# Hybrid GDN and MoBA layer: the keys of four heads in the first phase, and beta's and the decay's columns in the delta rule's gate

## Chip, cores and metric

The kernel runs on one core of a Trainium2 chip. The metric is device time in microseconds (us). Three executions of the kernel before took 785.45 to 785.89 us, median 785.75.

## The reference, cut to what matters

One layer: RMS norm of x (256 positions, 2048 channels, float32), one wide input projection, two token mixers (a gated delta rule with 8 heads of 128, and block attention with 8 heads of 128), their gates, a merge, an output projection, a norm and the residual. The change touches only the input side of the delta rule:

```python
SPLITS = (3 * GDN_WIDTH, GDN_WIDTH, GDN_HEADS, GDN_HEADS, 3 * MOBA_WIDTH, MOBA_WIDTH, D_MODEL, D_MODEL)
proj = h @ w_in
gdn_qkv, gdn_z, gdn_b, gdn_a, ... = jnp.split(proj, offsets, axis=-1)
qkv = jax.nn.silu(causal_depthwise_conv(gdn_qkv, conv_w))
beta = jax.nn.sigmoid(gdn_b)
g = -jnp.exp(a_log) * jax.nn.softplus(gdn_a + dt_bias)
oa = gated_delta_rule(qa, ka, va, beta, g)          # chunks of 64
oa = rms(oa) * gdn_norm_w * jax.nn.silu(gdn_z)
```

In w_in the 1024 columns of the gate z are followed directly by the 8 columns of beta and the 8 of the decay.

## The kernel before, in words

All matrix products with weights are done in three parts: a float32 weight tile is split into hi (a copy on ScalarE, L223) and lo (raw minus hi, on VectorE, L224), both in the fp32r format, and the input, transposed to hT, is kept as hi and lo too. TensorE (PE) adds hi by hi, hi by lo and lo by hi. `mm` (L140) and `tr` (L143) are the helpers through which every product and transpose goes, so all have these two lines; `pin` keeps them in the program's order, while the framework's scheduler may move unpinned instructions of the other engines.

`proj_n` makes a block of 512 output columns: positions on partitions, 16 input tiles (k) of 128 channels, two position halves, three products each: 96 products of 512 columns. `proj_t` makes two heads, channels on partitions: 16 tiles, two heads, one product of 512 columns (hi of the weight by hi and lo of the input) and one of 256: 64 products.

The first phase (up to L341) loads x and w_in's columns for the keys and queries of heads 0 and 1 in five pieces (CHUNKS: 2, 2, 4, 4, 4 tiles), transposes x (`turn`), scales it by the pre-norm weight into hT (`turned`), and multiplies the pieces as they land (`first_split`, `first_products`). `stats` sums x squared. A few products of ones (WARM, WARM2) run ahead of them. After the phase, pba multiplies hT by the 16 columns of beta and the decay, which came by their own transfer (wba) and stand split in a 64-column tile. a_log and dt_bias are broadcast from memory over 128 partitions; a part of the identity is written to memory (ident_d) and read back spread over partitions into tv, as the start of the inverse.

Then `ORDER` lists the blocks: mv, mk are attention, kq the keys and queries of two delta-rule heads, v their values, zg and zm the two gates, ga and gb the merge gates. In each block `tick` is called after every six products (proj_n) or four pairs (proj_t). A tick advances queues of generators, in which all other work waits: a step runs, then yields how many blocks of two ticks to wait. The delta rule's queue (gq) holds, one after the other, `decays` (softplus and cumulative sums pg, a write g_d and broadcast grow, exponentials of differences dec), `scores` of eight heads (11 ticks each), `inverse` (63 steps on VectorE, slower while a v block is recent) and `solve`. The first merge-gate block gb0 drains this queue when it ends.

VectorE, ScalarE, GpSimd (POOL) and SyncE (SP) issue in their own order. SP issues the weight loads, POOL the small and rearranging transfers. Raw weight tiles have three buffers, splits three, PSUM four banks for blocks (acc) and four for the rest (aux).

Of the kernel before, what the change touches and what calls it, by code (L numbers as in the profile page):

```python
# [15 lines left out]
P = 128  # L16
# [3 lines left out]
WARM = 4  # L20
# [4 lines left out]
D_WAIT = 3.5  # L25
# [14 lines left out]
    "mv0 kq1 kq2 zg0 kq3 zg1 v0 v1 v2 ga0 zm0 zm1 ga1 mv1 v3 ga2 ga3 mk0 mk1 gb0 mk2 gb1 mk3 gb2 gb3"  # L40
# [31 lines left out]
def hybrid_layer(  # L72
# [31 lines left out]
    CB = 4 * GW  # L104
    CMQ = CB + 2 * H
# [43 lines left out]
    CHUNKS = (0, 2, 4, 8, 12, KT)  # L149
    NCH = len(CHUNKS) - 1  # L150
    KC = 4
    pre = big.tile([P, KT * nba + P], F32, tag="ga", name="pre")
    wba = pre[:, : KT * nba].rearrange("p (k c) -> p k c", c=nba)
    prow = pre[:, KT * nba :]
    nrow = cst.tile([KT, P], F32, name="nrow")
    nc.gpsimd.dma_start(nrow, pre_norm_w.rearrange("o (k p) -> (o k) p", p=P))
    xs = [big.tile([P, D], F32, tag=("z0", "z1")[t], name=f"x_{t}") for t in range(NT)]
    FIRST = (("k", CK), ("q", CQ))
    rawf = {n: big.tile([P, KT, 256], F32, tag=f"g{i}", name=f"rawf_{n}") for i, (n, _) in enumerate(FIRST)}
    for c in range(NCH):  # L160
        cs = slice(CHUNKS[c] * P, CHUNKS[c + 1] * P)
        for t in range(NT):
            nc.sync.dma_start(xs[t][:, cs], xf[t * P : (t + 1) * P, cs])
        for n, col in FIRST:
            nc.sync.dma_start(
                rawf[n][:, CHUNKS[c] : CHUNKS[c + 1]], w_in[cs, col : col + 256].rearrange("(k p) c -> p k c", p=P)
            )
    nc.sync.dma_start(wba, w_in[:, CB : CB + nba].rearrange("(k p) c -> p k c", p=P))

# [10 lines left out]
    nc.gpsimd.dma_start(prow[0 : NTAP * NCV, :], conv_w.rearrange("o t (m p) -> (o t m) p", p=P))  # L180
    nc.gpsimd.dma_start(prow[NTAP * NCV : NTAP * NCV + 1, :], gdn_norm_w)
    na = cst.tile([P, H], F32, name="na")
    nc.gpsimd.dma_start(na, a_log.broadcast_to([P, H]))
    dtb = cst.tile([P, H], F32, name="dtb")
    nc.gpsimd.dma_start(dtb, dt_bias.broadcast_to([P, H]))
    wbs = big.tile([P, KT, 64], F32R, tag="tt", name="wbs")
    nc.gpsimd.memset(wbs.bitcast(F32), 0.0)
# [22 lines left out]
    sel = cst.tile([64, nba], F32, name="sel")  # L210
    ident_d = dram.tile([64, 64], F32, name="ident_d")
    nc.gpsimd.dma_start(ident_d, ident[0:64, 0:64])
# [20 lines left out]
    pfirst = {n: [acc_tile(f"a_{n}0_{m}") for m in range(2)] for n, _ in FIRST}  # L233

    def turn(c):

        ks = range(CHUNKS[c], CHUNKS[c + 1])
        each = 1 if len(ks) == 2 else 2
        pts = []
        for i, k in enumerate(ks):  # L240
            if i % each == 0:
                pt = aux_tile(f"hTp_{k}")
            pts.append(pt[:, (i % each) * S : (i % each + 1) * S])
            for t in range(NT):
                tr(pts[-1][:, t * P : (t + 1) * P], xs[t][:, k * P : (k + 1) * P], ident)
        return [(k, pts[i]) for i, k in enumerate(ks)]

    def turned(pts):
        for i in range(0, len(pts), 2):
            for k, pr in pts[i : i + 2]:  # L250
                pin(nc.scalar.activation(hT[:, k, :S], pr, AF.Copy, scale=ncol[:, k : k + 1]))
            for k, pr in pts[i : i + 2]:
                pin(
                    nc.vector.scalar_tensor_tensor(
                        hT[:, k, S:], pr, ncol[:, k : k + 1], hT[:, k, :S].bitcast(F32), op0=ALU.mult, op1=ALU.subtract
                    )
                )

# [13 lines left out]
    def first_split(n, c):  # L272
        hi = wspl.tile([P, KC, 256], F32R, tag="hi", name=f"hi_{n}0_{c}")
        lo = wspl.tile([P, KC, 256], F32R, tag="lo", name=f"lo_{n}0_{c}")
        for u in range(0, CHUNKS[c + 1] - CHUNKS[c], 2):
            us = slice(u, u + 2)
            raw = rawf[n][:, CHUNKS[c] + u : CHUNKS[c] + u + 2]
            pin(nc.scalar.copy(hi[:, us, :], raw))
            pin(nc.vector.tensor_tensor(lo[:, us, :], raw, hi[:, us, :].bitcast(F32), op=ALU.subtract))
        return hi, lo  # L280

    def first_products(n, c, hi, lo):
        for kk in range(CHUNKS[c + 1] - CHUNKS[c]):
            k = CHUNKS[c] + kk
            for m in range(2):
                ms = slice(m * P, (m + 1) * P)
                pt = pfirst[n][m]
                mm(pt, hi[:, kk, ms], hT[:, k, :], start=(k == 0), stop=False)
                mm(pt[:, :S], lo[:, kk, ms], hT[:, k, :S], start=False, stop=(k == KT - 1))

    pts = turn(0)
# [3 lines left out]
    turned(pts)  # L295
    for i in range(WARM2):
        mm(warm[:, :P], ones, ones, start=True, stop=True)
    sk_ = first_split("k", 0)
    for c in range(NCH):
        first_products("k", c, *sk_)  # L300
        if c == 0:
            pts = turn(1)
        sq_ = first_split("q", c)
        if c + 1 < NCH:
            turned(pts)
            sk_ = first_split("k", c + 1)
        if c > 1:
            stats(c - 2)
        first_products("q", c, *sq_)
        if c + 2 < NCH:  # L310
            pts = turn(c + 2)
    stats(3)

    pin(nc.scalar.copy(wbs[:, :, 0:nba], wba))
    pin(nc.vector.tensor_tensor(wbs[:, :, 32 : 32 + nba], wba, wbs[:, :, 0:nba].bitcast(F32), op=ALU.subtract))
    nc.vector.memset(sel, 0.0)
    nc.vector.tensor_copy(sel[0:nba, :], ident[0:nba, 0:nba])
    nc.vector.tensor_copy(sel[32 : 32 + nba, :], ident[32 : 32 + nba, 32 : 32 + nba])
# [23 lines left out]


# [18 lines left out]
    def proj_n(w, col, stat, nk, name):  # L362

        pts = [acc_tile(f"a_{name}_{t}") for t in range(NT)]
        for kb in range(nk // 4):
            raw = wraw.tile([P, 4, 512], F32, tag="raw", name=f"raw_{name}_{kb}")
            nc.sync.dma_start(raw, w[kb * 512 : (kb + 1) * 512, col : col + 512].rearrange("(k p) c -> p k c", p=P))
            for u in range(2):
                hi, lo = split(raw[:, 2 * u : 2 * u + 2, :], [P, 2, 512], f"{name}_{kb}_{u}")
# [12 lines left out]
    ba = big.tile([64, 2 * S], F32, tag="tv", name="ba")  # L382
    nc.scalar.copy(ba, pba[0:64, :])
# [9 lines left out]
    def decays():  # L393
        pbt = aux_tile("pbt")
        for t in range(NT):
            for half in range(2):
                o_ = half * S + t * P
                mm(
                    pbt[:, t * nba : (t + 1) * nba], ba[:, o_ : o_ + P], sel, start=(half == 0), stop=(half == 1)
                )  # L400
        zz = cst.tile([P, NT, H], F32, name="zz")
        sp = cst.tile([P, NT, H], F32, name="sp")
        for t in range(NT):
            pa_ = pbt[:, t * nba + H : (t + 1) * nba]
            pin(nc.vector.scalar_tensor_tensor(zz[:, t, :], pa_, rstd[:, t : t + 1], dtb, op0=ALU.mult, op1=ALU.add))
        for t in range(NT):
            pb_ = pbt[:, t * nba : t * nba + H]
            pin(nc.scalar.activation(beta[:, t, :], pb_, AF.Exp, scale=nrstd[:, t : t + 1]))
# [13 lines left out]
        for y in late:  # L422
            pin(nc.scalar.activation(y, y, AF.Silu))
# [50 lines left out]
    def conv_silu(y, m, late=None):  # L474
# [8 lines left out]
        if late is None:  # L483
            nc.scalar.activation(y, y, AF.Silu)
        else:
            late.append(y)
# [94 lines left out]
    def silu_gate(n, col, c):  # L581
        pts = proj_n(w_in, col + c * 512, hT, KT, f"{n}{c}")
        for t in range(NT):
            nc.scalar.activation(
                z_tiles[n]()[:, t, c * 512 : (c + 1) * 512], pts[t], AF.Silu, scale=rstd[:, t : t + 1]
            )

    def keys_queries(p):
        h = 2 * p
        pk = pfirst["k"] if h == 0 else proj_t(CK + h * P, f"k{h}")  # L590
        kTs = [halves(pk[m], f"k{h + m}") for m in range(2)]
        if h == 0:
            qTs = [halves(pfirst["q"][m], f"q{h + m}") for m in range(2)]
            gq.add(decays())
        for m in range(2):
            conv_silu(kTs[m], H + h + m, None if h else late)
        if h:
            pq = proj_t(CQ + h * P, f"q{h}")
            qTs = [halves(pq[m], f"q{h + m}") for m in range(2)]
        for m in range(2):  # L600
            conv_silu(qTs[m], h + m, None if h else late)
        for m in range(2):
            gq.add(scores(h + m, kTs[m], qTs[m]))
# [509 lines left out]
```

## Time and profile before

| What | us |
|---|---|
| median of three executions | 785.75 |
| the profiled execution | 785.95 |
| its span, first to last instruction | 784.2 |
| first product of the first phase | 6.89 |
| first product of the first mv block | 40.83 |
| first block of the branch outputs (ua), in the chain | 599.93 |

The profiled execution's time holds 1.75 us outside the span. In the profile, PE is TensorE's products, PEld its weight loads, DVE is VectorE, ACT ScalarE, POOL GpSimd; SPq is SyncE's queue. A row of a group of instructions names line, engine, operation, output and inputs, then shape, count, busy time and mean ns of one. Products overlap in the pipeline, so the distance between two starts, and not the mean duration, is what one costs.

### The profile page before, as it was taken

To read this page: it belongs to the slowest core of one execution; us is meant where nothing else is said; L and a number is where in the kernel's file an instruction comes from. 1 tells how busy PE (TensorE), PEld (TensorE's weight loads), DVE (VectorE), ACT (ScalarE), POOL (GpSimd) and SP (SyncE) were. 2 spreads that over 40 slices of the span, in tenths; PEclk is the share of its full clock that TensorE was granted. 3 is DMA by queue.
4 is the path that set the end of the run, shared out by engine and by line. 5 is a ranking of instruction groups with operands and counts; after the bars stand their busy time and mean duration, and the time that the engine had idled before them with its cause. 6 is when DMAs were issued, how large, how long until landed. Compare 5 with 4: busy or idle time off the path is not lost.

```text
span 784.2 us, 10150 instructions
## 1 busy us (share of the span) xinstructions
PE 771.6 (98%) x3869; PEld 647.9 (83%) x3869; DVE 531.9 (68%) x875; ACT 413.3 (53%) x624; POOL 26.2 (3%) x53
## 2 busy tenths in 40 slices
PE   8999999999999999999999999999999999999995
PEld 6878888888888888888888888888888888888884
DVE  4877886785867898874346466554645668986673
ACT  5777665554745545455354646454464445465451
POOL 3010000100110000020000000000000000000000
PEclk9999999999999999999999999999999999999999
DMA  8857655665596656686445465556456555577542
GB/s 261 261 160 215 189 187 165 197 189 162 175 267 218 213 163 212 190 235 191 117 127 163 160 214 161 169 165 204 162 166 230 195 185 206 196 271 268 167 156 107
DMA packets 95248, 149.77 MB, mean 191 GB/s; under 512 B 5152, under 2 KB 47184, under 8 KB 94560
## 3 DMA queue, kind: packets, MB, share of 16 engines
q1 hardware_dynamic: 92000, 136.46, 54.5%
q0 software_dynamic: 2624, 11.63, 5.2%
q10 hardware_dynamic: 576, 1.05, 0.4%
q8 instruction: 30, 0.49, 0.3%
q14 instruction: 18, 0.15, 0.1%
HBM read 145.95 MB, written 3.17 MB: 190 GB/s over the span
## 4 chain that ended last, share of the span: by engine, by line
PE 94%; DVE 2%; SPq 1%; ACT 1%; DMA 1%; issue 0%; DVEq 0%; ACTq 0%
PE a_ga L140 11%; PE a_gb L140 11%; PE a_y L140 11%; PE a_mk L140 6%; PE a_v L140 6%; PE a_mq L140 6%; PE a_zg L140 6%; PE a_zm L140 6%; PE a_q L140 5%; PE a_k L140 5%; PE a_ub L140 5%; PE a_mv L140 5%; PE a_ua L140 5%; PE sv L140 2%; PE s L140 1%; DMA x<-in_x_dram 1%
## 5 line engine op out<-in xcount | busy, mean ns | idle before, releaser
L140 PE MATMUL a_ga<-hi_ga,hT 128*128 128x512 f32 x256 | 82.2, 394 | 0.0
L140 PE MATMUL a_gb<-hi_gb,hT 128*128 128x512 f32 x256 | 82.1, 394 | 0.0
L224 DVE TENSOR_TENSOR lo_gb<-raw_gb,hi_gb 128x1024 fp32r<-128x1024 f32 x32 | 39.2, 1224 | 41.1 <-ACT hi_gb L223 41.1
L223 ACT CAST hi_gb<-raw_gb 128x1024 fp32r<-128x1024 f32 x32 | 33.7, 1052 | 48.5 <-PE a_gb L140 34.5
L224 DVE TENSOR_TENSOR lo_ga<-raw_ga,hi_ga 128x1024 fp32r<-128x1024 f32 x32 | 39.0, 1223 | 29.2 <-ACT hi_ga L223 29.1
L223 ACT CAST hi_ga<-raw_ga 128x1024 fp32r<-128x1024 f32 x32 | 33.5, 1050 | 46.1 <-PE a_ga L140 30.3
L140 PEld LDWEIGHTS a_ga<-hi_ga,hT 128*128 128x128 f32 x256 | 48.1, 188 | 11.0 <-issue 1.0
L140 PEld LDWEIGHTS a_gb<-hi_gb,hT 128*128 128x128 f32 x256 | 48.1, 188 | 10.0
L140 PE MATMUL a_ga<-lo_ga,hT 128*128 128x512 f32 x128 | 50.0, 391 | 0.0
L140 PE MATMUL a_gb<-lo_gb,hT 128*128 128x512 f32 x128 | 49.8, 389 | 0.0
L140 PE MATMUL a_k<-hT,hi_k 128*128 128x512 f32 x128 | 46.8, 406 | 0.1
L140 PE MATMUL a_mk<-hT,hi_mk 128*128 128x512 f32 x128 | 46.1, 401 | 0.0
L140 PE MATMUL a_mq<-hT,hi_mq 128*128 128x512 f32 x128 | 45.7, 400 | 0.0
L140 PE MATMUL a_y<-hi_y,mT 128*128 128x512 f32 x144 | 45.6, 390 | 0.0
L140 PE MATMUL a_q<-hT,hi_q 128*128 128x512 f32 x128 | 45.6, 397 | 0.0
L140 PE MATMUL a_v<-hT,hi_v 128*128 128x512 f32 x128 | 45.3, 397 | 0.0
L140 PE MATMUL a_ua<-hi_ua,oaT 128*128 128x512 f32 x128 | 41.8, 395 | 0.0
L140 PE MATMUL a_zg<-hi_zg,hT 128*128 128x512 f32 x128 | 40.6, 391 | 0.0
L140 PE MATMUL a_zm<-hi_zm,hT 128*128 128x512 f32 x128 | 40.6, 392 | 0.0
L140 PE MATMUL a_mv<-hi_mv,hT 128*128 128x512 f32 x128 | 40.5, 392 | 0.0
L140 PE MATMUL a_ub<-hi_ub,obT 128*128 128x512 f32 x128 | 40.0, 389 | 0.0
L140 PE MATMUL a_k<-hT,lo_k 128*128 128x256 f32 x128 | 36.4, 284 | 0.0
(333 smaller groups left out, 1906.5 us busy)
## 6 DMA issues: line engine op xcount, KB each, us to landing
raw_ga<-in_w_in_dram SPq DMA_DIRECT2D x16, 1024.0 KB, 5.2
raw_gb<-in_w_in_dram SPq DMA_DIRECT2D x16, 1024.0 KB, 5.1
raw_y<-in_w_out_dram SPq DMA_DIRECT2D x15, 1024.0 KB, 5.0
raw_mv<-in_w_in_dram SPq DMA_DIRECT2D x8, 1024.0 KB, 5.6
raw_zg<-in_w_in_dram SPq DMA_DIRECT2D x8, 1024.0 KB, 5.1
raw_v<-in_w_in_dram SPq DMA_DIRECT2D x8, 1024.0 KB, 5.7
raw_zm<-in_w_in_dram SPq DMA_DIRECT2D x8, 1024.0 KB, 5.3
raw_mq<-in_w_in_dram SPq DMA_DIRECT2D x8, 1024.0 KB, 5.7
```

The costliest lines, as they stand in the source:

```text
L140: return pin(nc.tensor.matmul(*args, **kwargs))
L223: nc.scalar.copy(hi, raw)
L224: nc.vector.tensor_tensor(lo, raw, hi.bitcast(F32), op=ALU.subtract)
```

## The change

The first phase loads the keys of heads 0 to 3 (512 columns) instead of keys and queries of heads 0 and 1, in four pieces of four tiles each; x lands in pieces of 512 columns, the keys one tile of 128 rows and 512 columns per transfer. The number of the phase's products is the same: 64 of 512 columns and 64 of 256. Queries of heads 0 and 1, and 2 and 3, become blocks q0 and q1 of the order. pba and what fed it are gone: the gate zg is made in three blocks of 348, 348 and 344 columns, the last of which holds the gate's last 328 columns and the 16 of beta and the decay. This third block runs first, ahead of the order, in aux banks, and `decays` reads its last columns. a_log and dt_bias are one row, spread over partitions by a product with ones. tv is made by GpSimd (a memset and four selects). The small loads move from GpSimd's queue to SP's, nrow ahead of x and the others behind the keys. WARM is 6 instead of 4, D_WAIT 7 instead of 3.5.

```diff
-WARM = 4
+WARM = 6
-D_WAIT = 3.5
+D_WAIT = 7
-    "mv0 kq1 kq2 zg0 kq3 zg1 v0 v1 v2 ga0 zm0 zm1 ga1 mv1 v3 ga2 ga3 mk0 mk1 gb0 mk2 gb1 mk3 gb2 gb3"
+    "q0 mv0 zg0 q1 kq2 kq3 zg1 v0 v1 v2 ga0 zm0 zm1 ga1 mv1 v3 ga2 ga3 mk0 mk1 gb0 mk2 gb1 mk3 gb2 gb3"
...
+    ZG = (0, 348, 696, GW + nba)
+    ZW, ZBA = ZG[3] - ZG[2], GW - ZG[2]
+    NCH = KT // 4
-    nc.gpsimd.dma_start(nrow, pre_norm_w.rearrange("o (k p) -> (o k) p", p=P))
+    nc.sync.dma_start(nrow, pre_norm_w.rearrange("o (k p) -> (o k) p", p=P))
+    rawk = [big.tile([P, KT // 2, 512], F32, tag=f"g{i}", name=f"rawf_k{i}") for i in range(2)]
     for c in range(NCH):
-        cs = slice(CHUNKS[c] * P, CHUNKS[c + 1] * P)
         for t in range(NT):
+            cs = slice(c * 512, (c + 1) * 512)
             nc.sync.dma_start(xs[t][:, cs], xf[t * P : (t + 1) * P, cs])
-        for n, col in FIRST:
-            nc.sync.dma_start(
-                rawf[n][:, CHUNKS[c] : CHUNKS[c + 1]], w_in[cs, col : col + 256].rearrange("(k p) c -> p k c", p=P)
-            )
-    nc.sync.dma_start(wba, w_in[:, CB : CB + nba].rearrange("(k p) c -> p k c", p=P))
+        for k in range(4 * c, 4 * c + 4):
+            nc.sync.dma_start(rawk[k // 8][:, k % 8], w_in[k * P : (k + 1) * P, CK : CK + 512])
...
-    nc.gpsimd.dma_start(na, a_log.broadcast_to([P, H]))
-    nc.gpsimd.dma_start(dtb, dt_bias.broadcast_to([P, H]))
+    adrow = cst.tile([1, nba], F32, name="adrow")
+    nc.sync.dma_start(adrow[:, :H], a_log)
+    nc.sync.dma_start(adrow[:, H:], dt_bias)
-    nc.gpsimd.dma_start(ident_d, ident[0:64, 0:64])
...
+    def first_split(k, n):
+        hi = wspl.tile([P, 2, 512], F32R, tag="hi", name=f"hi_k0_{k}")
+        lo = wspl.tile([P, 2, 512], F32R, tag="lo", name=f"lo_k0_{k}")
+        raw = rawk[k // 8][:, k % 8 : k % 8 + n]
+        pin(nc.scalar.copy(hi[:, :n], raw))
+        pin(nc.vector.tensor_tensor(lo[:, :n], raw, hi[:, :n].bitcast(F32), op=ALU.subtract))
+        return [(k + i, hi[:, i], lo[:, i]) for i in range(n)]
+    def first_products(parts):
+        for k, hi, lo in parts:
+            for part in range(2):
+                for m in range(4):
+                    ms, pt = slice(m * P, (m + 1) * P), pfirst[m]
+                    if part == 0:
+                        mm(pt, hi[:, ms], hT[:, k, :], start=(k == 0), stop=False)
+                    else:
+                        mm(pt[:, :S], lo[:, ms], hT[:, k, :S], start=False, stop=(k == KT - 1))
...
+    turned(pts[:2])
+    parts = first_split(0, 1) + first_split(1, 1)
+    turned(pts[2:])
+    parts += first_split(2, 2)
     for c in range(NCH):
+        first_products(parts[4 * c : 4 * c + 2])
+        if c + 1 < NCH:
+            turned(turn(c + 1))
         if c == 0:
+            parts += first_split(4, 2)
+        stats(c)
+        first_products(parts[4 * c + 2 : 4 * c + 4])
+        for k in (4 * c + 6, 4 * c + 8):
+            if k < KT:
+                parts += first_split(k, 2)
-    pba = aux_tile("pba")
-    for k in range(KT):
-        mm(pba[0:64, :], wbs[:, k, :], hT[:, k, :], start=(k == 0), stop=(k == KT - 1))
...
+    mm(pcp[:, P : P + nba], ones[0:1, :], adrow, start=True, stop=True)
+    nc.vector.tensor_copy(nad, pcp[:, P : P + nba])
...
     def decays():
-        pbt = aux_tile("pbt")
...
+        pbt = [pt[:, ZBA:ZW] for pt in pzg]
...
+        nc.gpsimd.memset(tv, 1.0)
         for g in range(4):
-            nc.gpsimd.dma_start(
-                tv[32 * g : 32 * g + 32],
-                ident_d.rearrange("(c g) i -> g c i", g=4)[g].unsqueeze(0).broadcast_to([32, 16, 64]),
+            nc.gpsimd.affine_select(
+                out=tv[32 * g : 32 * g + 32],
...
-    keys_queries(0)
+    pzg = proj_n(w_in, CZ + ZG[2], hT, KT, "zg2", ZW, aux_tile)
+    late.append(lambda: silu_out("zg", ZG[2], GW, pzg))
+    gq.add(decays())
+    for m in range(4):
+        conv_silu(kTs[m // 2][m % 2], H + m, late)
```

More of the change, by code (lines that the diff above doesn't have):

```diff
@@ L270, in stats @@
                 )
[L272 to L291, printed above, removed]
+    def first_split(k, n):
[12 more added lines that the diff above has]
+                        mm(pt, hi[:, ms], hT[:, k, :], start=(k == 0), stop=False)
+                    else:
+                        mm(pt[:, :S], lo[:, ms], hT[:, k, :S], start=False, stop=(k == KT - 1))
     pnc = aux_tile("pnc")
@@ L421, in decays @@
         yield 0.5
-        for y in late:
-            pin(nc.scalar.activation(y, y, AF.Silu))
+        for f in late:
+            f()
         yield PG_WAIT
@@ L485, in conv_silu @@
         else:
-            late.append(y)
+            late.append(lambda: pin(nc.scalar.activation(y, y, AF.Silu)))
     HG = H // 2
@@ L579, in hybrid_layer, with silu_out, silu_gate, keys @@
     zg, zm = z_tiles["zg"], z_tiles["zm"]
-    def silu_gate(n, col, c):
-        pts = proj_n(w_in, col + c * 512, hT, KT, f"{n}{c}")
+    def silu_out(n, c0, c1, pts):
         for t in range(NT):
-            nc.scalar.activation(
-                z_tiles[n]()[:, t, c * 512 : (c + 1) * 512], pts[t], AF.Silu, scale=rstd[:, t : t + 1]
-            )
-    def keys_queries(p):
-        h = 2 * p
[L590 to L594, printed above, removed]
+            pin(
+                nc.scalar.activation(
+                    z_tiles[n]()[:, t, c0:c1], pts[t][:, : c1 - c0], AF.Silu, scale=rstd[:, t : t + 1]
+                )
+            )
+    def silu_gate(n, c):
+        c0, c1 = (ZG[c], ZG[c + 1]) if n == "zg" else (c * 512, (c + 1) * 512)
+        silu_out(n, c0, c1, proj_n(w_in, {"zg": CZ, "zm": CMZ}[n] + c0, hT, KT, f"{n}{c}", c1 - c0))
+    kTs = [[] for _ in range(H // 2)]
+    def keys(p):
+        pk = proj_t(CK + 2 * p * P, f"k{2 * p}")
+        kTs[p] += [halves(pk[m], f"k{2 * p + m}") for m in range(2)]
+        for m in range(2):
+            conv_silu(kTs[p][m], H + 2 * p + m)
+    def queries(p):
+        h = 2 * p
+        pq = proj_t(CQ + h * P, f"q{h}")
+        qTs = [halves(pq[m], f"q{h + m}") for m in range(2)]
         for m in range(2):
[L596 to L599, printed above, removed]
+            conv_silu(qTs[m], h + m)
         for m in range(2):
-            conv_silu(qTs[m], h + m, None if h else late)
-        for m in range(2):
-            gq.add(scores(h + m, kTs[m], qTs[m]))
+            gq.add(scores(h + m, kTs[p][m], qTs[m]))
         if p == H // 2 - 1:
```

114 lines of the change are left out of this document (43 added, 71 removed).

## The prediction, made before the changed kernel ran

> **What bounds the kernel now.** I read the page first: its totals, then the chain that ended last.
>
> ```profile
> span 784.2 us, 10150 instructions
> PE 771.6 (98%) x3869; PEld 647.9 (83%) x3869; DVE 531.9 (68%) x875; ACT 413.3 (53%) x624; POOL 26.2 (3%) x53
> ...
> PE 94%; DVE 2%; SPq 1%; ACT 1%; DMA 1%; issue 0%; DVEq 0%; ACTq 0%
> ```
>
> The matmul engine is busy for 98% of the span and makes 94% of the chain. So time is won by fewer or shorter matmuls, or by closing PE's few holes; work on other engines counts only where PE waits for it. The view of waits, PE alone, names all the holes that have a releaser:
>
> ```profile
> PE hTp L143 <- DMA x<-in_x_dram: 2.2, 4, 1.2
> PE warm L140 <- DVE epst L177: 1.1, 1, 1.1
> PE pg L140 <- DVE sp L415: 0.9, 1, 0.9
> ```
>
> The change touches the first and the third; four of hTp's are counted, 0.37 us of them at 4.13. Next, the chain in order of time, from 36 to 45 us, shows what PE does between the first phase and the first block of the order:
>
> ```profile
> 36.60 3.68 PE pba L140 x16
> 40.28 0.44 PE prr L140 x4
> 40.72 0.11 PE pcp L143
> 40.83 1.38 PE a_mv L140 x6
> 42.21 0.99 PE pbt L140 x8
> ```
>
> **Part 1: beta's and the decay's own products go.** The 16 products pba (3.68 us) and the 8 small ones pbt (0.99 us) are on PE, on the path, and nothing replaces them as instructions: **-4.7 us**. One product of adrow is added, like half of prr's four records: **+0.2 us**.
>
> **Part 2: the gate blocks.** The delta rule's gate takes 96 products in each of two blocks of 512 columns now; it will take 96 in each of three blocks of 348, 348 and 344 columns, 288 in all. No row shows a width of 348. These are the neighbours (the chain around 112 to 136 us, then the whole chain's list):
>
> ```profile
> 121.16 1.03 PE s L140 x6
> ...
> 123.80 12.27 PE a_zg L140 x54
> ```
>
> ```profile
> 65.58 11.29 PE a_k L140 x64
> ```
>
> A 512-wide product costs 12.27/54 = 227 ns. The six of s are three of 512 and three of 256 columns, each with weights of its own: (1.03 - 3 x 0.227)/3 = 116 ns for 256. On the line through both points 348 columns cost 116 + 92 x 0.434 = 156 ns and 344 cost 154. The row of a_k gives 11.29/32 = 353 ns for a pair of 512 and 256, so 126 ns for the 256, and then 348 cost 162. In proportion to the width it would be 154. So 288 products take 44.4 to 46.6 us, against 192 x 0.227 = 43.6 us now. I take 45.2, between the two readings: **+1.6 us**, ends +0.8 and +3.0. The Trainium skill (TensorE: Matmul & The Clock Gate, section Back-to-back issue gap) gives N/2.4 + 2.5 ns, an estimate of 147 ns for 348 columns, and by that price the blocks would cost -1.2 us and the total would be 2.8 us lower. Its own value for 512 is 216 ns, where the row has 227, so the rows decide.
>
> Splits go on feeding this. A split of 1024 elements takes DVE 1.22 us and ACT 1.05 us (rows below) for 12 products of 227 ns, 2.7 us. For 696 elements, in proportion, that is 0.83 us for 1.9 us of products: covered the same way.
>
> ```profile
> L140 PEld LDWEIGHTS a_zg<-hi_zg,hT 128*128 128x128 f32 x128 | 24.0, 188 | 5.0
> L224 DVE TENSOR_TENSOR lo_zg<-raw_zg,hi_zg 128x1024 fp32r<-128x1024 f32 x16 | 19.6, 1223 | 5.7 <-ACT hi_zg L223 5.6
> L223 ACT CAST hi_zg<-raw_zg 128x1024 fp32r<-128x1024 f32 x16 | 16.9, 1053 | 15.2 <-PE a_zg L140 9.4 <-PE a_q L140 5.0 <-ACT kq L514 0.6
> ```
>
> **Part 3: the first phase.** Its products are as many as before: 64 of 512 columns, 64 of 256, 32 transposes. What can change is the wait for x, and the start. The chain shows what undisturbed work costs, eight transposes and then half of four input tiles' products:
>
> ```profile
> 24.63 0.87 PE hTp L143 x8
> 25.50 2.78 PE a_k L140 x16
> ```
>
> The timeline of PE shows the start:
>
> ```profile
> 4.13 0.90 PE L143 MATMUL hTp<-ident,x 128*128 128x128 f32 x3 [0.37 <-DMA x<-in_x_dram]
> ...
> 5.18 1.65 PE L140 MATMUL warm<-ones 128*128 128x128 f32 x6
> ...
> 6.89 0.80 PE L140 MATMUL a_k<-hT,hi_k 128*128 128x512 f32 x1
> ...
> 9.81 0.60 PE L143 MATMUL hTp<-ident,x 128*128 128x128 f32 x4
> ```
>
> The first product starts at 6.89, and from there all products (8 x 2.78 = 22.2) and 28 transposes (28 x 0.11 = 3.1) would end at 32.2. They end at 36.60. Of the 4.4 us lost, PE waits 1.8 for x (2.2 less the 0.37 ahead of the first product); the rest is the early clock, about half speed (three transposes take 0.90 us at 4.13, four take 0.60 at 9.81), and refills after each wait. Why x is late shows in two stretches and one row of the DMA list:
>
> ```profile
> 6.00:9.00 3.00, 2.94 (x9) 2.08 (x9) 2.25 (x4) 1.36 (x3) 1.83 (x8) 1.00 0.83 133
> 9.00:12.00 3.00, 2.82 (x16) 2.21 (x14) 1.26 (x3) 1.35 (x3) 0.00 (x0) 1.00 1.03 317
> ```
>
> ```profile
> ident_d<-ident POOLq DMA_DIRECT2D x1, 16.0 KB, 7.2
> ```
>
> From 6 to 9 us the DMA engines are 0.83 busy and move 133 GB/s, against 317 at 1.03 right after: 0.55 MB behind, 1.7 us. The small transfers of POOL's queue run in that stretch; one of 16 KB took 7.2 us to land. The change drops ident_d's write, the broadcasts of a_log and dt_bias and the fetch of wba, and sends the other small ones behind the big loads. x and the keys are the same 6.3 MB; at 317 GB/s that is 20 us, and PE needs 25 for the phase.
>
> The start: nrow goes ahead of x on SP, and x's first piece is twice as large. SP's own rows in the chain:
>
> ```profile
> 4.67 0.47 SPq L163
> ...
> 5.19 1.77 SPq L163
> ...
> 7.00 2.08 SPq L165
> ```
>
> One more issue is 0.47 us at most, and 256 KB more ahead of x's second half take up to 0.8 us at 317 GB/s, less what the halved packets cost now: x is whole near 4.8 us instead of 4.13. Then the eight transposes and six warm records stand ahead of the first product at 0.21 each (transposes x3 in 0.90): 4.8 + 14 x 0.21 = 7.8 us. The two more loops of WARM (0.9 us) lie in the wait before. The five small transfers that SP now issues behind the big ones (some 0.47 us each) stand ahead of the gate's weights, which are wanted ten microseconds later. If the clock is up by 9.7 us, as it is in the row of 9.81, half speed costs (9.7 - 7.8)/2 = 1.0. So the products end at 7.8 + 22.2 + 24 x 0.11 + 1.0 = 33.6, with 0.4 for refills 34.0, instead of 36.60: **-2.6 us**. Ends: -3.6 (x by 4.1) and 0 (x by 5.5 and waits for pieces as now).
>
> **Part 4: what waits for beta.** pg waits 0.9 us for sp in the first mv block, because the gate's exponentials queue behind convolutions. In the change zg's third block (15 us) lies between the keys and the decays, pg is due eight ticks into q0 (11 us), and most of the four convolutions are done by then: **-0.9 us**, ends 0 and -0.9. The two banks of that block stay held until the late SiLUs; pg and pgt have the other two.
>
> **Part 5: the chain behind the decays.** Queued steps fall on ticks, one each six products (or four pairs). Counted from the waits in the code, the inverse's loads come at tick 119 instead of 112, its last step at 213 instead of 209 (slow steps behind v3), the first solve product at 231 instead of 227, and the last transposes at 285, the end of gb0, in both. These rows give the slack:
>
> ```profile
> L638 DVE TENSOR_TENSOR tw<-lc,tv x63: 184/368/450, 242.0 to 338.3; 128x252 f32<-128x252 f32 x3, 128x60 f32<-128x60 f32 x2, 128x112 f32<-128x112 f32 x2, 128x156 f32<-128x156 f32 x2
> ```
>
> ```profile
> L143 PE MATMUL ot<-ident,os x16: 270/272/273, 420.2 to 473.3; 128*128 128x128 f32 x16
> ```
>
> Five microseconds later is still inside the same blocks, and the outputs are wanted only by ua: **0**. tv's memset and selects are on POOL, which is idle (26.2 us in all), long ahead of 242 us: 0.
>
> What is new is DVE's load in zg0: the decay's differences (below) now fall into a block with short products.
>
> ```profile
> L447 DVE SCALAR_TENSOR_TENSOR dec<-grow,gcol,mask_t x16: 342/345/347, 65.1 to 71.2; 128x128 f32<-128x128 f32 x16
> ```
>
> 16 x 0.345 us and four sums (some 1.7 us) are 7.2, about three quarters of them in zg0: 5.4, with 8 splits of 0.83 (6.6) and one head's scores (some 3) 15.0 us of DVE in 15 us of PE. Buffers for three splits hide most of it. I take **+0.5 us**, ends 0 and +2.5.
>
> **Sum.** -4.7 + 0.2 + 1.6 - 2.6 - 0.9 + 0 + 0.5 = -5.9 us. The profiled execution took 785.95 us (span 784.2 and 1.75 around it): 780.05; the median of the runs shown is 785.75, 0.2 lower, so 779.85, say **779.9 us**. Differences under 0.2% (1.6 us) can hardly be told from none.
>
> **Rivals.**
> The first loads stay late: 24 large transfers go through SP, whose own issues at 5.19 and 7.00 were held up for 1.77 and 2.08 us, and if that and not POOL's transfers made the slump, the 2.6 us stay: 782.5. For it: the hold-up lies in the same stretch. Against: DMA engines busy at 0.83 with 133 GB/s, so not short of orders. Chance 0.15.
> DVE becomes the bound in the narrow blocks (zg0, and zg1 with two heads' scores): 2 us more, 781.9. For it: 15 of 15 us. Against: this stretch, with four blocks, the decay and scores, in which PE is never idle with DVE at 41.3 of 47.4 us. Chance 0.13.
>
> ```profile
> 65.40:112.80 47.40, 47.40 (x274) 41.35 (x273) 41.29 (x89) 31.77 (x55) 0.00 (x0) 1.00 0.61 186
> ```
>
> The clock rises later: PE idles between the first warm products and x, and one more stretch as long as the slow products now (6.89 to about 9.7, and a little over) at half speed costs some 1.7 us: 781.6. The Trainium skill (same page, section What's actually happening) says that the gate judges free-running windows of about 3.4 us; slow rows until 6.89 and fast ones at 9.81 agree with it, but no row shows the windows. Chance 0.07.
> Slower: a product of the narrow blocks costs its weight load. LDWEIGHTS lasts 188 ns; if loads don't overlap one another, 288 x 0.188 = 54.1 us, +10.5 in place of +1.6: 788.8. It decides from (43.6 + 7.5)/288 = 177 ns for each product. Against it: s's 256-wide products at 116 ns with loads of the same size. For it: no long run of narrow products is in the trace. Chance 0.10.
> Better: PE's clock or the first x comes earlier and the widths cost 154 ns: 778. Chance 0.07.
> The forecast, 778.6 to 781.4: chance 0.48.
>
> **Range and chances.** All good ends together give 777.5 us, all bad ones without the weight loads 786.8, but they need four failures at once. 777.5 to 784.0 us leaves out the slower case and little else. Faster by over 0.2% (below 784.2): 0.86; within: 0.04; slower: 0.10.
>
> **What would show it.** In the changed kernel's chain the gate's rows should read near 156 ns a product; near 188 the slower rival holds. PE's waits should have no hTp after the first product and no pg; an hTp wait after 10 us says that the loads stayed late. The first block after the keys should start near 34.8 us instead of 40.83 (pba 3.7, part 3's 2.6, adrow). New idle PE in zg0 or zg1 behind DVE's lo_zg would be the second rival. The forecast would be wrong altogether if the delayed inverse stretched into a wait of PE for os or tt.

## The result, and the profile after

| | before | after |
|---|---|---|
| median of 20 executions, us | 785.59 | 783.61 |
| lowest and highest, us | 784.87 to 786.02 | 782.01 to 785.47 |
| profiled execution, us | 785.95 | 784.95 |
| its span, us | 784.2 | 783.2 |

The ratio after to before is 0.9975, with a 95% interval of 0.9968 to 0.9982: a gain of 2.0 us where 5.9 were forecast. The profiled execution of after lies in the upper part of its 20, so its span shows a gain of 1.0 us only. The spread is new too: 3.5 us after, 1.2 before.

The page's totals of after, and its chain that ended last by engine:

```profile
span 783.2 us, 10314 instructions
...
PE 770.1 (98%) x3947; PEld 656.7 (84%) x3947; DVE 530.1 (68%) x874; ACT 412.2 (53%) x624; POOL 24.6 (3%) x47
...
PE 91%; DVE 3%; ACT 2%; DMA 2%; issue 1%; SPq 0%; DVEq 0%; ACTq 0%
```

PE's busy time fell by only 1.5 us, though 4.7 us of products went, and its share of the chain fell from 94% to 91%: the three points went to DVE, ACT and DMA, which were at 2, 1 and 1%. PE's waits in after:

```profile
PE hTp L142 <- DMA x<-in_x_dram: 1.4, 2, 0.9
PE pcp L139 <- DVE pcol L320: 1.1, 1, 1.1
PE warm L139 <- DVE epst L173: 1.1, 1, 1.1
PE a_zm L139 <- DVE lo_zm L214: 0.8, 1, 0.8
PE a_zg L139 <- DVE lo_zg L214: 0.5, 1, 0.5
```

pg's wait and the waits for x after the first product are gone, as forecast. Three waits are new: pcp (the PSUM tile of the small parameters, into which adrow's product goes too), a_zm and a_zg (products of two gate blocks). The chain in order of time, up to the first block (start, us, what):

```profile
1.71 4.37 DMA x<-in_x_dram
...
6.12 1.75 PE hTp L142 x7
7.88 1.28 PE warm L139 x6
9.16 4.11 PE a_k L139 x16
...
14.14 5.61 PE a_k L139 x32
...
36.77 0.33 DVE rrow L316
37.10 0.21 DVE pcol L320
...
37.35 0.39 PE pcp L139 x2
37.74 12.34 PE a_zg L139 x77
```

The first block starts at 37.74, where the forecast had 34.8 and before 40.83. Read the first product row against the later one: sixteen products take 4.11 us, and further on thirty-two take 5.61, 2.8 for sixteen. PE's timeline shows where that changes:

```profile
8.81 2.05 PE L139 MATMUL a_k<-hT,hi_k 128*128 128x512 f32 x4
...
11.52 1.29 PE L139 MATMUL a_k<-hT,hi_k 128*128 128x512 f32 x4
```

The trace's clock record begins full speed at 11.94 us. Ahead of its first entry it holds nothing, and there the windows below show a clock of 1.00, though the products run at about half speed.

The transfer rate at the start, in four windows of 1 us (the last number is GB/s), says why x is whole only at 6.1 us and not at 4.8:

```profile
2.00:3.00 1.00, 1.00 (x7) 1.00 (x6) 0.00 (x0) 0.28 (x2) 1.00 (x7) 1.00 0.31 99
3.00:4.00 1.00, 1.00 (x6) 0.78 (x5) 0.00 (x0) 0.00 (x0) 0.93 (x2) 1.00 0.94 246
4.00:5.00 1.00, 0.53 (x3) 0.35 (x2) 0.17 (x1) 0.00 (x0) 0.94 (x2) 1.00 0.76 170
5.00:6.00 1.00, 0.22 (x1) 0.00 (x0) 0.00 (x0) 0.00 (x0) 1.00 (x1) 1.00 0.82 256
```

I had priced 256 KB more at 317 GB/s; in this stretch, in which the keys' first transfers run too, the mean is 193.

The timeline of ScalarE at the end of zg0, then that of PE, shows the hole of a_zg:

```profile
88.75 0.78 ACT L213 CAST hi_zg<-raw_zg 128x696 fp32r<-128x696 f32 x1 [0.56 <-PE a_zg L139]
89.55 1.28 ACT L441 ACT_TABLE_LOAD   x1
90.84 3.05 ACT L441 ACTIVATE dec<-dec 128x768 f32<-128x768 f32 x4
93.80 2.10 ACT L213 CAST hi_zg<-raw_zg 128x696 fp32r<-128x696 f32 x3
```

```profile
90.31 0.48 PE L139 MATMUL a_zg<-hi_zg,hT 128*128 128x348 f32 x2
...
90.79 0.48 PE L139 MATMUL a_zg<-hi_zg,hT 128*128 128x348 f32 x2
...
94.16 0.88 PE L139 MATMUL a_zg<-hi_zg,hT 128*128 128x348 f32 x2
...
95.52 0.43 PE L139 MATMUL a_zg<-lo_zg,hT 128*128 128x348 f32 x1 [0.49 <-DVE lo_zg L214]
```

A table load and the four exponentials of the decay hold ScalarE for 4.3 us in a row; the splits come late, and by the distances of the products' ends PE loses 0.40 us inside the pair at 94.16 (0.88 for 0.48) and 0.76 at 95.52: 1.16 in all. The first two rows give the narrow width: three products in 0.48 us, 160 ns each.

The third new hole, 1.04 us by the ends of the products, is at 241.5. PE waits there for zm's first splits and ScalarE for zm's first weights, and the broadcast of lc (issues; transfers to landing) lies ahead of it:

```profile
241.53 0.50 PE L139 MATMUL a_zm<-lo_zm,hT 128*128 128x512 f32 x1 [0.76 <-DVE lo_zm L214]
```

```profile
239.16 2.00 ACT L213 CAST hi_zm<-raw_zm 128x1024 fp32r<-128x1024 f32 x2 [5.78 <-DMA raw_zm<-in_w_in_dram]
```

```profile
L620 POOL DMA_DIRECT2D lc<-l_d x4: 489/496/518, 220.8 to 222.3; - x4
...
DMA to landing us min/median/max: 8.8/11.8/14.7
```

Part 5 had put the later inverse at no cost. lc is issued at 220.8, 4.6 us ahead of raw_zm's first transfer (in before 9.4 us), and the slowest transfer of raw_zm takes 9.8 us where the median one takes 5.2. That lc makes it late is not shown: in e3, e6 and e7 below, lc comes 4.1, 4.5 and 3.9 us ahead, and there is no such hole.

### The profile page after: what moved, and what is told of

It reads as the page before. It is cut to its first block, busy times and chain, and to the rows that moved or that the text cites. A ratio compares the mean times of both kernels' runs of the same rounds, so it can differ in the third digit from the quotient of the medians.

```text
span 783.2 us, 10314 instructions
## 1 busy us (share of the span) xinstructions
PE 770.1 (98%) x3947; PEld 656.7 (84%) x3947; DVE 530.1 (68%) x874; ACT 412.2 (53%) x624; POOL 24.6 (3%) x47
## 4 chain that ended last, share of the span: by engine, by line
PE 91%; DVE 3%; ACT 2%; DMA 2%; issue 1%; SPq 0%; DVEq 0%; ACTq 0%
PE a_gb L139 11%; PE a_y L139 11%; PE a_ga L139 9%; PE a_mq L139 6%; PE a_mk L139 6%; PE a_v L139 6%; PE a_k L139 6%; PE a_zm L139 6%; PE a_mv L139 5%; PE a_ub L139 5%; PE a_zg L139 5%; PE a_ua L139 5%; PE a_q L139 4%; DMA raw_zm<-in_w_in_dram 2%; PE sv L139 2%; PE s L139 1%
## 5 line engine op out<-in xcount | busy, mean ns | idle before, releaser
L139 PE MATMUL a_zg<-hi_zg,hT 128*128 128x348 f32 (+1 forms) x192 | 47.5, 323 | 0.1
L139 PE MATMUL a_k<-hT,hi_k 128*128 128x512 f32 x128 | 41.3, 406 | 0.0
L139 PE MATMUL a_mq<-hT,lo_mq 128*128 128x256 f32 x128 | 35.9, 281 | 0.0
```

Of the source, the lines that this page charges most:

```text
L139: return pin(nc.tensor.matmul(*args, **kwargs))
```

## The experiments

Each was run five to twelve times beside runs of before on the same chip; ratios are to before, with a 95% interval. Each has one profiled execution.

**e1_adrow: adrow's product ahead of pcol's copy.** Both results lie in one PSUM tile, and the product waited for the copy.

```diff
-    nc.vector.tensor_copy(pcol, pcp[:, :P])
     mm(pcp[:, P : P + nba], ones[0:1, :], adrow, start=True, stop=True)
+    nc.vector.tensor_copy(pcol, pcp[:, :P])
```

> The changed kernel with one line moved: adrow's product stands ahead of pcol's copy, which uses the same PSUM bank. Theory (the gain was eaten by new holes of PE): PE no longer waits 1.1 us for pcol, so about 1.1 us less than the changed kernel's 783.6, 782.5. Rival (the hole only covers the gate block's first splits, which are late anyway): PE waits for lo_zg in its place and the time stays at 783.6.

Measured: 782.73 us, 0.9967 (0.9955 to 0.9979). Its chain:

```profile
6.11 0.56 PE hTp L142 x3
...
8.22 3.05 PE a_k L139 x16
...
33.59 0.63 PE prr L139 x4
34.22 0.11 PE pcp L142
34.33 0.32 PE pcp L139 x2
34.65 5.40 PE a_zg L139 x33
```

From prr (four products that lay the norm's factor of every position across all partitions) to the first block it is 1.06 us now, against 2.26 in after, whose phase ends at 35.48: the wait was worth 1.2. The 1.2 rests on the profiles; the medians differ by 0.9, and their intervals overlap. The profile shows a second difference, which the edit doesn't explain: up to 6 us this kernel issues what after does, yet its sixteen products take 3.05 us, not 4.11. The clock record begins full speed at 4.74 us here, at 11.94 in after's profile (and at 9.64 in that of e2, below, with the same start). With that the block starts at 34.65, where the forecast had 34.8, though by another sum: the forecast had the clock up at 9.7 us and adrow's product cheaper.

**e3_warm11: WARM 11 in place of 6**, so that PE is never idle before x is whole.

```diff
-WARM = 6
+WARM = 11
```

> The changed kernel with WARM 11 instead of 6, so that PE has work from 1.1 us until x is whole near 6.1. Theory (the idle stretch from 4.2 to 6.1 us costs the clock one window, and the different runs differ by it): the clock is up before the first product near 8.5, the time falls by 1 to 1.7 us to about 782.3, and the runs lie closer than the changed kernel's 782.0 to 785.5. Rival (the clock comes when it comes): 783.6, same spread.

Measured: 781.86 us (781.59 to 782.09), 0.9955 (0.9942 to 0.9967). The chain has no wait for x:

```profile
1.12 4.53 PE warm L139 x22
...
8.18 3.06 PE a_k L139 x16
```

The gain is 1.75 us at the median, and the spread falls from 3.5 us (20 executions) to 0.5 (5). In the profiles of all seven kernels here with WARM 9 or 11 (e3, e6, e7, e8, e10, e12, e15) full speed begins between 4.35 and 7.25 us, ahead of the first product. With WARM 6 it begins at 4.74, 9.64 and 11.94 in e1, e2 and after, and the phase ends at 33.59, 34.49 and 35.48. So the start of the clock moves the end of the phase by 1.9 us between these three, more than half of after's spread. It need not be the whole 1.75 us: the hole in zm, too, stands in the profiles of after, e1 and e2 and in none of those seven. Why that is so stays open, and one profile of each kernel can't part the two.

**e6_warm_adrow: both edits.**

```diff
-WARM = 6
+WARM = 11
...
-    nc.vector.tensor_copy(pcol, pcp[:, :P])
     mm(pcp[:, P : P + nba], ones[0:1, :], adrow, start=True, stop=True)
+    nc.vector.tensor_copy(pcol, pcp[:, :P])
```

> WARM 11 and adrow's product ahead of pcol's copy, both. Theory: the two holes are independent, 781.9 less 1.2 is 780.7. Rival (PE then waits for the gate's first splits, or reaches the first zm block earlier and meets its late load again): 781.5 or more.

Measured: 780.73 us, 0.9939 (0.9926 to 0.9952), as expected: the two edits' gains are separate, and add up. Of the three new waits zg0's alone is left.

**e7_exps: e6 with the exponentials spread**, one behind the next pair of heads' differences.

```diff
+            if h:
+                pin(nc.scalar.activation(dec[:, h - 2 : h, :], dec[:, h - 2 : h, :], AF.Exp))
             yield 1
-        for h in range(0, H, 2):
-            pin(nc.scalar.activation(dec[:, h : h + 2, :], dec[:, h : h + 2, :], AF.Exp))
+        pin(nc.scalar.activation(dec[:, H - 2 :, :], dec[:, H - 2 :, :], AF.Exp))
```

> As the kernel with WARM 11 and adrow moved, and the four exponentials of the decay issued one behind each pair of heads instead of four in a row. Theory (four exponentials and a table, 4.3 us in a row on ScalarE, outlast the three split buffers of a narrow block): PE's wait for lo_zg in zg0 goes, 1.2 us less, 779.5. Rival (the block wants more than ScalarE and VectorE can give, whatever the order): the wait stays, 780.7.

Measured: 780.06 us, 0.9930 (0.9918 to 0.9942). The hole of a_zg is gone from the waits, and zg0, from its first product to that of the next block, takes 16.52 us instead of 17.65 in e6. The gain of 0.7 us at the median is less than these 1.1; where the rest went isn't known.

**e2_swap: q1 ahead of zg0 in the order**, so that the exponentials fall into wide products.

```diff
-    "q0 mv0 zg0 q1 kq2 kq3 zg1 v0 v1 v2 ga0 zm0 zm1 ga1 mv1 v3 ga2 ga3 mk0 mk1 gb0 mk2 gb1 mk3 gb2 gb3"
+    "q0 mv0 q1 zg0 kq2 kq3 zg1 v0 v1 v2 ga0 zm0 zm1 ga1 mv1 v3 ga2 ga3 mk0 mk1 gb0 mk2 gb1 mk3 gb2 gb3"
```

> The changed kernel with q1 ahead of zg0 in the order, so that the exponentials of the decay (4.3 us of ScalarE with their table) fall into a block whose splits last 2.8 us and not 1.9. Theory (ScalarE, not VectorE, starves the narrow block): the 1.2 us of PE's wait for lo_zg near 95 us go, nothing comes in their place, 782.4. Rival (VectorE's load is what counts, and q1 with its convolutions loads it more): the wait moves into q1 or stays, 783.6 or more.

Measured: 783.57 us, 0.9974 (0.9964 to 0.9983): no gain. zg0's hole is gone, but mv0 now waits 0.7 us for lo_mv at 81 us, and zm's hole is 0.56 + 1.04. The load was moved, not hidden.

**e4_phase: the first phase without the gate part** (pba, pbt and the gate's two blocks of 512 columns as before); the edit is to the changed kernel, whose order, WARM 6, adrow's product and tv by GpSimd stay.

```diff
+    nc.sync.dma_start(wba, w_in[:, CB : CB + nba].rearrange("(k p) c -> p k c", p=P))
...
+    for k in range(KT):
+        mm(pba[0:64, :], wbs[:, k, :], hT[:, k, :], start=(k == 0), stop=(k == KT - 1))
...
-    pzg = proj_n(w_in, CZ + ZG[2], hT, KT, "zg2", ZW, aux_tile)
```

> The first phase of the changed kernel alone: keys of four heads, but beta and the decay by the old product pba and the gate in two blocks of 512 columns. Theory: against the changed kernel pba and pbt cost 4.7 us more, the gate 2.3 less, the holes at adrow (1.3) and in zg0 (1.2) go, a wait for sp of up to 0.9 returns: 783.5 to 784.4. Rival (the narrow blocks cost more than their rows say, and all the gain is the first phase's): 782 or less. Second rival (the first phase gains nothing): 785.6 or more.

Measured: 786.00 us, 1.0009 (1.0000 to 1.0018). The phase's products end 1.65 us earlier, but pcp waits 0.6, pg 0.7, and the new queries block has a hole of 0.46. As the second rival had it, the new phase brings nothing by itself. It still carries adrow's wait here, and its clock record begins full speed at 10.69 us; with the edits of e1 and e3 it wasn't run.

**e5_gate and e9_gate_d7: the gate part alone** on the kernel before, with D_WAIT 3.5 and 7; tv is still loaded by transfers. The edit is to the kernel before.

```diff
-    nc.sync.dma_start(wba, w_in[:, CB : CB + nba].rearrange("(k p) c -> p k c", p=P))
...
-    for k in range(KT):
-        mm(pba[0:64, :], wbs[:, k, :], hT[:, k, :], start=(k == 0), stop=(k == KT - 1))
-    ba = big.tile([64, 2 * S], F32, tag="tv", name="ba")
-    nc.scalar.copy(ba, pba[0:64, :])
...
+            pzgs.append(proj_n(w_in, CZ + ZG[2], hT, KT, "zg2", ZW, aux_tile))
```

> The kernel before with the gate part alone: pba, pbt and wba go, the gate is made in blocks of 348, 348 and 344 columns, the last of them (with beta and the decay) ahead of the order; the first phase, its loads and WARM stay as before. Theory (this part carries the gain, the new first phase gives it back through its late start): against before -4.7 for pba and pbt, -0.9 for pg's wait, +2.3 for the narrower blocks: 782.3. Rival (the narrow blocks starve in other places too and cost what pba did): 785 or more.

> The gate part alone as in the run of 791.1 us, with D_WAIT 7. Theory (what made that run slow is the decay's differences, issued before grow had landed: VectorE waits, PE idles 2.4 us and then runs 3.4 us at half clock): with seven ticks more the wait and the half clock go, and the part brings what its products say, -4.7 - 0.9 + 2.3 against before: 782.1, up to 783.5 with small holes. Rival (the narrow blocks are at fault): 787 or more.

Measured: 791.11 us, 1.0081 (1.0063 to 1.0100), and 791.42, 1.0079 (1.0066 to 1.0091): both theories failed by 8 to 9 us, and the rivals' bounds held. Two things show in e9. The loads of tv, first in before and then in e9 (issues, ns, first and last start):

```profile
L618 POOL DMA_DIRECT2D tv<-ident_d x4: 651/656/705, 43.8 to 45.8; - x4
```

```profile
L605 POOL DMA_DIRECT2D tv<-ident_d x4: 648/656/702, 12.6 to 14.6; - x4
```

In before their buffer was taken by ba until 43.8 us; with ba gone they start at once and run among x's pieces. And in e9 the exponentials fall between SiLUs of a key block, with a table load at every change, and behind them the clock falls (windows: PE's busy time, then the granted clock third from the end):

```profile
92.89 1.28 ACT L444 ACT_TABLE_LOAD   x1
94.18 0.85 ACT L444 ACTIVATE dec<-dec 128x768 f32<-128x768 f32 x1
95.03 1.28 ACT L464 ACT_TABLE_LOAD   x1
96.33 0.72 ACT L464 ACTIVATE y_k<-y_k 128x256 f32<-128x256 f32 x2
97.06 1.28 ACT L444 ACT_TABLE_LOAD   x1
98.35 2.31 ACT L444 ACTIVATE dec<-dec 128x768 f32<-128x768 f32 x3
```

```profile
100.00:103.43 3.43, 0.50 (x1) 0.19 (x1) 2.48 (x5) 3.43 (x7) 0.00 (x0) 1.00 0.30 107
103.43:106.84 3.41, 3.28 (x10) 2.88 (x11) 3.39 (x8) 1.40 (x3) 0.00 (x0) 0.50 0.17 24
```

ScalarE is held for 7.8 us, PE loses 2.56 + 1.33 us ahead of 104, and the next 3.41 us run at a granted clock of 0.50, an estimate of 1.7 us more (half of them).

**e13_gate_tv: e9 with tv made by GpSimd**, as in the full change.

```diff
-    nc.gpsimd.dma_start(ident_d, ident[0:64, 0:64])
...
+        nc.gpsimd.memset(tv, 1.0)
         for g in range(4):
-            nc.gpsimd.dma_start(
+            nc.gpsimd.affine_select(
+                out=tv[32 * g : 32 * g + 32],
...
```

> The gate part alone with D_WAIT 7, and the inverse's start tv made by GpSimd as in the full change. In the run without that (791.4 us) the four loads of tv (128 KB each, 256 bytes a row) were issued at 12.6 us, in the first phase, where the kernel before issues them at 43.8 us, because the buffer that held them back is gone; PE waited 3.0 us for x there, two holes of 1.47 and 1.27 us at 25 and 26 us, and the phase ended at 38.76 (before: 36.60). Theory: these loads make that wait. Without them the phase ends at 36.3 to 37.2 us and the time is 789.2 to 790.0. Rival: x is late because the gate's weights are issued in the same stretch; then the phase still ends at 38 or later and the time stays above 790.5.

Measured: 788.36 us, 1.0040 (1.0027 to 1.0053): 3.1 us less than e9, more than the theory gave; the phase ends at 36.23 instead of 38.76. Two windows of e9, then the same of e13 (last number GB/s):

```profile
18.00:21.00 3.00, 3.00 (x20) 2.67 (x19) 2.10 (x5) 1.46 (x4) 0.00 (x0) 1.00 1.08 198
21.00:24.00 3.00, 2.84 (x17) 2.23 (x15) 0.55 (x1) 1.21 (x3) 0.00 (x0) 1.00 1.07 262
```

```profile
18.00:21.00 3.00, 3.00 (x21) 2.68 (x20) 2.45 (x6) 2.79 (x7) 0.00 (x0) 1.00 1.07 366
21.00:24.00 3.00, 3.00 (x19) 2.58 (x18) 2.75 (x6) 1.48 (x4) 0.00 (x0) 1.00 1.08 356
```

The DMA engines are equally busy and move 168 GB/s less in the first of them. There e9's transfers from GpSimd's queue, tv's, move 0.30 MB in 52% of the engines' time and SP's 0.29 MB in 55%; in e13 SP's move 1.10 MB in 107%. So both tv's bytes and those beside them take about twice the engines' time. That tv's source rows of 256 bytes are the reason is not shown. Nor is all of the loss explained: behind e13's phase the exponentials still fall between SiLUs, and its clock record has 3.41 us of 0.50 from 100.62 us on, as e9's has.

**e14_gate_tv_order: e13 with zg0 right behind mv0.**

```diff
-    "mv0 kq1 kq2 zg0 kq3 zg1 v0 v1 v2 ga0 zm0 zm1 ga1 mv1 v3 ga2 ga3 mk0 mk1 gb0 mk2 gb1 mk3 gb2 gb3"
+    "mv0 zg0 kq1 kq2 kq3 zg1 v0 v1 v2 ga0 zm0 zm1 ga1 mv1 v3 ga2 ga3 mk0 mk1 gb0 mk2 gb1 mk3 gb2 gb3"
```

> As the kernel of e13_gate_tv, with zg0 right behind mv0 in the order (mv0 zg0 kq1 kq2). Theory: what is left of the loss comes from where the decay's exponentials fall, between the SiLUs of a key block: ScalarE runs table loads of 1.28 us and exponentials for 7.8 us, PE waits 3.9 us, and the clock is at half for 3.4 us behind it (1.7 us lost). In zg0 no SiLU stands between them and the hole is near the full change's 1.2 us: the time is 783.3 to 785.0. Rival: the loss is in the gate part itself (widths, buffers), and the time stays at 788 or more.

Measured: 786.37 us (784.79 to 789.00), 1.0018 (1.0007 to 1.0029): between theory and rival. The clock doesn't fall, but in its profile zg0 still loses 1.5 us, the key block 2.2 and zm 1.6. The new place of zg0 is worth 2.0 us at the median, in executions that spread over 4.2 us and with intervals that just overlap; the rest of the gate part's loss is in further waits that I haven't taken apart.

**e15_tv_back: e7 with tv loaded by transfers again**, the opposite of e13.

```diff
+    nc.gpsimd.dma_start(ident_d, ident[0:64, 0:64])
...
-        nc.gpsimd.memset(tv, 1.0)
         for g in range(4):
-            nc.gpsimd.affine_select(
+            nc.gpsimd.dma_start(
+                tv[32 * g : 32 * g + 32],
+                ident_d.rearrange("(c g) i -> g c i", g=4)[g].unsqueeze(0).broadcast_to([32, 16, 64]),
```

> The opposite of e13_gate_tv: the kernel of e7_exps (780.06 us), with tv loaded by four transfers from a copy of the identity, as before the change, and made by GpSimd no more. Their buffer is free from the start, so they fall into the first phase. Theory: PE waits 1.3 to 2.5 us for x or the keys there, the phase ends at 35.5 to 36.7 instead of about 34.4, and the time is 781.4 to 782.6. Rival: the new phase, with fewer small transfers, has room for 0.5 MB more, and the time stays within 0.5 us of 780.1.

Measured: 782.25 us, 0.9960 (0.9947 to 0.9973): 2.2 us more than e7, inside the theory's range. The phase ends at 36.39, against 33.72 in e7, behind a hole of 1.6 us for x at 19.2:

```profile
12.00:15.00 3.00, 3.00 (x19) 2.64 (x18) 2.30 (x5) 2.94 (x7) 0.00 (x0) 1.00 1.05 218
15.00:18.00 3.00, 2.81 (x17) 2.22 (x15) 1.20 (x3) 0.09 (x1) 0.00 (x0) 1.00 1.05 199
```

The same windows of e7 move 397 and 382 GB/s. So in both directions tv by GpSimd is a needed part of the change, worth 2 to 3 us.

**e8_piece, e10_nrow, e12_nrow_piece: an earlier start.** e8 is e6 with WARM 9 and x's first piece of 256 columns; e10 is e7 with nrow on GpSimd's queue; e12 has all of these.

```diff
-WARM = 11
+WARM = 9
...
+            if k in (0, 2) or (c and k == 4 * c):
+                cs = slice(k * P, k * P + (512 if c else 256))
+                for t in range(NT):
+                    nc.sync.dma_start(xs[t][:, cs], xf[t * P : (t + 1) * P, cs])
...
-    nc.sync.dma_start(nrow, pre_norm_w.rearrange("o (k p) -> (o k) p", p=P))
+    nc.gpsimd.dma_start(nrow, pre_norm_w.rearrange("o (k p) -> (o k) p", p=P))
```

> As the kernel with adrow moved, WARM 9, and x's first piece halved: 256 columns of both halves, two tiles of keys, the next 256 columns, two tiles. Theory (the first product waits for 512 KB of x at the slow rate of the first microseconds): x's first piece is whole near 4.6 instead of 6.1 us, the first product starts near 7.0 instead of 8.2, and the time is 1 to 1.2 us below the 780.7 of the kernel without it: 779.6. Rival (the first transfers are late whatever their size): 780.7.

> As the kernel of 780.06 us (WARM 11, adrow moved, exponentials spread), and nrow again on GpSimd's queue, so that x is SyncE's first transfer. Theory (nrow's issue delays x by its own 0.45 us): x whole near 5.7 instead of 6.1, first product near 7.9, 779.6. Rival (the first transfers are slow whatever stands ahead of them, or nrow now comes late and the scale waits): 780.1 or more.

> As the kernel with nrow on GpSimd's queue, with x's first piece of 256 columns and WARM 9. Theory (with nothing ahead and half the bytes, x comes as early as in the kernel before): x whole near 4.5, first product near 6.9, 778.7. Rival (the phase's end is set by splits or later pieces, not by its start, as the halved piece alone showed no gain): 779.6 to 780.1.

Measured: 781.03 us, 0.9945 (0.9933 to 0.9957); 780.63, 0.9936 (0.9924 to 0.9949); 779.66, 0.9927 (0.9914 to 0.9941). In e8 the first product comes at 7.7 us instead of 8.6, but the products end at 34.07 instead of 34.02, so the earlier start is lost again within the phase. All three theories failed. None of the three gains over e6 or e7 beyond the intervals. e12 is the fastest version, 5.9 us under before; e7 can't be told from it.

**e11_before_warm: before with WARM 7 in place of 4.**

```diff
-WARM = 4
+WARM = 7
```

> The kernel before with WARM 7 instead of 4: its only change. Theory (the early clock is worth the same there: PE idles from 3.2 to 4.1 us, and filling that stretch brings the clock up before the first products): clock up by about 6 to 7 us instead of 9.7, 1 to 1.4 us less, 784.2. Rival (before's clock is not held back by that gap): 785.4.

Measured: 785.39 us, 1.0002 (0.9993 to 1.0011): nothing. The clock record of its profile begins full speed at 3.98 us instead of 9.66, but the products end at 36.11 instead of 36.60: PE runs ahead and waits 1.4 us for x at 12.5. So an early clock alone gains nothing in before, where the phase hangs on x's transfers.

## Why the prediction was right in kind and wrong in size

**Part 1.** The 4.7 us of pba and pbt went. "One product of adrow is added, like half of prr's four records: +0.2 us" failed. The product stands behind pcol's copy, which stands behind lo_zg and rrow on VectorE (chain of after, 36.77 to 37.35). From the end of the phase to the first block it is 2.26 us, where before has 0.55 beside pba: adrow cost 1.7. I named no queue for this step; the wait is 1.2 of it (e1), the product itself 0.5.

**Part 2.** The mechanism held. 348 columns cost 160 ns, near the 162 that I had read from the pairs of a_k, not my 156: 96 x (2 x 160 + 158) ns = 45.9 us, so +2.3 where I took +1.6. A product starts every 160 ns though each has a weight load of 188 ns: the slower rival is dead. The formula of the Trainium skill (TensorE: Matmul & The Clock Gate, section Back-to-back issue gap), 147 ns for 348 columns, which the page gives for a product by itself, doesn't agree with these rows.

**Part 3** failed as much as adrow's term, by 1.5 us: -2.6 forecast, -1.1 in the profile (the phase ends at 35.48, in before at 36.60). "x is whole near 4.8 us" was 6.1. The two costs that I named, 0.47 and 0.8, would have made it 5.4 in full, and I took 0.67 of them; at 193 GB/s, not the 317 of a later stretch, 256 KB take 1.36 us, and with nrow's issue of 0.44 and before's 4.13 that gives 5.9. So the first product came at 8.81, not 7.8: 1.0 us. "If the clock is up by 9.7 us" was 11.94 in this execution: 11.94 - 8.81 = 3.1 us at half speed cost 1.6 where I had 1.0. What I took for one number was 4.74, 9.64 and 11.94 in three profiles with the same start. The rest of the part held: behind the first product PE waits for x no more.

**Part 4** held: pg's wait is gone.

**Part 5.** The load in zg0 was +1.16, where I took +0.5 with VectorE as the late engine; it was ScalarE, with the four exponentials and the table load that I hadn't counted. The later chain cost 1.0 in zm in this profile, where I took 0: I checked the deadlines of the inverse, and not what its transfers run beside. e3, e6 and e7 show no hole in zm, so this term isn't a fixed price of the later inverse, and its cause stays open.

**The sum** by the profile: first block 40.83 to 37.74, -3.1; pbt -1.0; pg -0.9; widths +2.3; zg0 +1.2; zm +1.0: -0.5, against -1.0 of the span; 0.5 us stays unassigned. Of 5.9 us forecast, 1.5 were lost to x and the clock, 1.5 to adrow, 0.7 to the widths, 0.7 to zg0 and 1.0 to zm, 5.4 in all; the unassigned 0.5 is on the other side. The experiments confirm the three that I could mend: with WARM 11, adrow's order and the spread exponentials the time is 780.06 us, and the forecast was 779.9. That these two agree so well is luck in part: the widths still cost 0.7 more, and the 1.0 that the forecast had for half speed is gone (e7's clock record begins at 4.35 us, its first product at 8.28).

**Rivals.** The third (the clock rises later, 781.6) is what happened in part, at a chance of 0.07; the first holds for the very start only; the second named the right place and the wrong engine. The measured 783.61 lies in the range, near its upper end: no rival came true in full, but five terms were missed by 0.7 to 1.5 us each.

**What I took for separate terms isn't separate.** Alone, the phase gains nothing (e4) and the gate part loses 5.8 us (e9): taking pba away also frees the buffer that kept tv's loads out of the first phase, and pushes the exponentials into whatever block is next. In the full change GpSimd makes tv, and the new order puts zg0 there. My sum ran over terms of the full change, so it didn't fail by that, but neither half, as it was run, would have been kept alone.

## What to carry to other kernels

A product or copy that is added between two phases costs its place in the queues, and a PSUM tile that it shares, more than its own duration: name what it stands behind. A buffer that goes away also releases the transfers that waited for it; ask when they now start. And where the first products run before the clock has risen, keep the matmul engine busy until the first data are there, as in e3; it gains nothing where transfers set the pace behind them, as in e11.

## What the runs showed of the hardware

The moment of full speed ranged from 3.98 to 11.94 us, and between two kernels with the same first 6 us it was 4.74 and 11.94. In e9 a window of 3.43 us with PE busy for 0.50 was followed by 3.41 us at a granted clock of 0.50, and in e13 one of 3.42 with 0.70; so were two places in e5, with a hole of 2.4 us and with holes of 1.45 and 1.03 us close together, while the holes of after, e1 and e14 (0.5 to 1.5 us, and in e14 0.7 and 1.0 close together) were not. The Trainium skill (same page, section What's actually happening) tells of free-running windows of 3413 ns, judged busy or idle; the 3.41 us and the draw at the start agree with it. Its remark there, that the ramp costs less than 1% of a typical kernel's span, agrees as well, but the 1.75 us that e3 gained, 0.2%, are nearly as much as the change itself had brought.
